# The second group of a pointwise convolution: two of its eight pairs by seven products

## The chip, the cores and the metric

The kernel runs on one core of one Trainium2 chip. The metric is the device time of one execution in microseconds; the median of several is taken. Beside it stands one execution recorded by the hardware profiler, whose span goes from the first instruction to the last.

## What is computed

One layer of a hybrid encoder block in float32, for 256 tokens and a model width of 4096. Cut to what matters here:

```python
proj = rms_norm(x) @ w_in                       # 4096 -> 14336: q k v z_a a_c g_c z_c
y_a  = rms_norm(chunked_attention(q, k, v)) * silu(z_a)
u    = silu(layer_norm(depthwise_conv(a_c * sigmoid(g_c))))
y_c  = rms_norm(u @ w_pw + b_pw) * silu(z_c)    # w_pw: 2048 x 2048, the pointwise convolution
h    = x + concat(y_a, y_c) @ w_out
h    = h + sigmoid(rms_norm(h) @ w_ple_gate + b) * (p @ w_ple)
out  = rms_norm(h)
```

The change lies in `u @ w_pw + b_pw`.

## The kernel before

**Products.** Every float32 operand is split into a high part (a cast, on ScalarE, L204) and a low part (a subtraction on VectorE, L205). A product of a block of 128 activations by 128 x 512 weights is three matmuls on TensorE: high by high, low by high, high by low.

**Groups and pairs.** `mixed_product` (L340 on) computes a group: two halves of tokens (h = 0, 1) by two stretches of 512 columns (j = 0, 1), in four accumulator banks. It goes over the contraction in pairs of 128-row blocks, in the order that `order` gives. For a *plain* pair, both blocks are multiplied into all four banks: 2 x 4 x 3 = 24 matmuls. For a pair marked `*`, the 2 x 2 x 2 block product is done with seven products instead of eight (L452 to L488): 7 x 3 = 21 matmuls. It needs sums of the weights (ua at L465 and L466, ub at L472 and L473, on VectorE), the parts of these sums (uh on ScalarE, ul on VectorE), and sums of the activations that are made beforehand, here called combinations (`combine_again`, L287; its last steps are L276 on ScalarE and L277 on VectorE). P1 and three helper products, P5, P6 and P7, go into four helper banks, and when the last such pair of a group is through, `on_helpers` adds them up (L509 to L513, and lines of the caller).

**Buffers.** Weights arrive by SyncE's queue in five buffers `w`; wh and wl have three each, ua/ub, uh and ul two each. The queue issues a load when VectorE has read the tile that held the buffer before.

**The pointwise convolution.** L996 to L1032: two groups (columns 0 to 1023 and 1024 to 2047), eight pairs each. The activations are uS[0] to uS[3], two pairs in each. uC holds the combinations of pairs 0 and 2, made ahead of the first group. The first group takes pairs 0 and 2 by seven products; the second takes all pairs plain and has no helper sums, so it adds the bias with the last sums (L1030).

**What follows.** `xS` (L1037 on) are six more combinations, of the normalised input, for the gate groups that come next (order `dense`: 1 0\* 3 2\* 5 4\* 6\* 7 8\* ...). Their tiles xS[1] to xS[3] come from the pool `more`, whose four tiles are uS[0] to uS[3], so each waits until the second pointwise group is done with one of these.

**Order of the work.** The order of instructions on each engine is made at compile time: an instruction goes when its operands and its buffers are free in the compiler's model of the time, and among those that can go, the earlier line of the program goes first. Each engine then works through its list in that order. Only the instructions under `pin` keep the order of the program, and there are none of these around the change.

Of the kernel before, what the change touches and what calls it, by code (L numbers as in the profile page):

```python
# [25 lines left out]
def hybrid_block(  # L26
# [297 lines left out]
    def units(text):  # L324

        return [(int(u.rstrip("*+")), u[-1] if u[-1] in "*+" else "") for u in text.split()]
# [666 lines left out]

    fill(len(later))

    point = units("1 3 4 5 0* 6 2* 7"), units("0 1 2 3 4 5 6 7")  # L996
    uC = {}
    for c in range(2):
        uC[2 * c] = act.tile([P, 2, 2, T], F32R, tag="act", name="comb_u"), 0
# [339 lines left out]
```

## Time and profile before

| | |
|---|---|
| median of 3 runs | 2033.08 us (2032.29 to 2034.44) |
| profiled execution | 2032.83 us, span 2031.1 us |
| granted TensorE clock | 0.998 of full |
| first pointwise group | about 900 to 947 us |
| second pointwise group | about 947 to 990.5 us |
| first gate group | from 991.0 us |

Times in the views are microseconds from the start of the span. PE is TensorE, PEld its weight loads, DVE VectorE, ACT ScalarE, SP SyncE. A line of the timeline has start, duration, engine, line of the kernel, operation, output and inputs, and in brackets how long the engine sat idle before it and what ended that. L204 and L205 are helpers that every weight tile goes through; the names tell which tile it is: wh and wl of the weights, uh and ul of their sums.

### The profile page before, as it was taken

Reading aid. Unit: us, or ns where it says so; the run is one execution under the profiler, and the core shown is the slowest. Engines: PE = TensorE matmul, PEld = TensorE weight load, DVE = VectorE, ACT = ScalarE, POOL = GpSimd, SP = SyncE. Lnnn points to the kernel's source line nnn. Section 1 sums busy time; section 2 is a strip of 40 time slices with the busy share of each in tenths; the row PEclk is TensorE's granted clock in tenths of the full one; section 3 lists DMA queues with packets and bytes.
Section 4 is the critical chain, followed back from the end, with each engine's and each line's share of the span. In section 5 each row is a group of like instructions: output and inputs, shape, how many; then the busy total and the mean of one; then the engine's idle time right before and its main releaser. Section 6 shows DMA issues by size and latency. Waiting matters only on the chain.

```text
span 2031.1 us, 26144 instructions
## 1 busy us (share of the span) xinstructions
PE 2015.5 (99%) x9094; PEld 1658.7 (82%) x9094; DVE 1871.1 (92%) x2658; ACT 1203.3 (59%) x1568; POOL 46.0 (2%) x50
## 2 busy tenths in 40 slices
PE   9999999999999999999999999999999999999997
PEld 7888888888888888888888888888888888888876
DVE  7999999679999986868899999999999999999998
ACT  7655555655655445676556566675665666665555
POOL 0000000000000000000000000000000000000000
PEclk9999999999999999999999999999999999999999
DMA  8787878688678867556666666676666656666765
GB/s 294 223 237 233 257 214 251 191 245 239 188 217 250 254 187 207 171 185 205 194 214 198 202 205 214 217 229 209 206 213 201 208 187 207 204 220 205 234 208 179
DMA packets 171167, 436.69 MB, mean 215 GB/s; under 512 B 13966, under 2 KB 17182, under 8 KB 171034
## 3 DMA queue, kind: packets, MB, share of 16 engines
q1 hardware_dynamic: 161952, 417.93, 64.0%
q0 software_dynamic: 8432, 16.25, 4.9%
q8 instruction: 71, 1.16, 0.2%
q10 hardware_dynamic: 650, 0.84, 0.1%
q14 instruction: 62, 0.51, 0.1%
HBM read 430.77 MB, written 4.19 MB: 214 GB/s over the span
## 4 chain that ended last, share of the span: by engine, by line
PE 92%; DVE 5%; issue 2%; ACT 1%; DMA 1%; POOLq 0%; POOL 0%; ACTq 0%; DVEq 0%
PE acc L383 67%; PE acc_P L383 16%; PE acc L229 5%; DVE wl L205 2%; PE tmp_ps L170 1%; DVE cv L721 1%; DMA wt<-in_w_out_dram 0%; PE tmp_ps L890 0%; DVE ul L205 0%; PE tmp_ps L874 0%; PE tmp_ps L908 0%; PE tmp_ps L913 0%; ACT wh L204 0%; PE acc L371 0%; DVE cv L799 0%
## 5 line engine op out<-in xcount | busy, mean ns | idle before, releaser
L383 PE MATMUL acc<-wh,big_t 128*128 128x512 f32 x3992 | 1234.7, 391 | 0.7 <-DVE y_c L1030 0.3
L204 ACT CAST wh<-wt 128x1024 fp32r<-128x1024 f32 (+1 forms) x737 | 713.4, 978 | 550.5 <-PE acc L383 365.0
L205 DVE TENSOR_TENSOR wl<-wt,wh 128x1024 fp32r<-128x1024 f32 (+1 forms) x737 | 821.8, 1127 | 82.0 <-ACT wh L204 78.6
L383 PEld LDWEIGHTS acc<-wh,big_t 128*128 128x128 f32 x3992 | 746.8, 188 | 155.1 <-issue 0.9
L383 PE MATMUL acc<-wl,big_t 128*128 128x512 f32 x1996 | 770.7, 391 | 0.6 <-DVE wl L205 0.5
L383 PEld LDWEIGHTS acc<-wl,big_t 128*128 128x128 f32 x1996 | 374.3, 188 | 79.5 <-DVE wl L205 2.3
L204 ACT CAST uh<-ua 128x1024 fp32r<-128x1024 f32 x160 | 168.3, 1052 | 80.9 <-DVE ua L466 46.1
L721 DVE SCALAR_TENSOR_TENSOR cv<-uT,dw,cv 128x250 f32<-128x250 f32 (+19 forms) x480 | 202.3, 463 | 1.1
L205 DVE TENSOR_TENSOR ul<-ua,uh 128x1024 fp32r<-128x1024 f32 x160 | 194.9, 1218 | 8.4 <-ACT uh L204 8.0
L383 PE MATMUL acc_P<-uh,big_t 128*128 128x512 f32 x516 | 157.9, 391 | 0.0
L204 ACT CAST uh<-ub 128x1024 fp32r<-128x1024 f32 x92 | 96.8, 1053 | 95.8 <-DVE ub L473 86.5
L205 DVE TENSOR_TENSOR ul<-ub,uh 128x1024 fp32r<-128x1024 f32 x92 | 112.2, 1220 | 6.1 <-ACT uh L204 5.2
L383 PEld LDWEIGHTS acc_P<-uh,big_t 128*128 128x128 f32 x516 | 95.8, 188 | 22.3 <-ACT uh L204 3.1
L383 PE MATMUL acc_P<-ul,big_t 128*128 128x512 f32 x258 | 98.8, 391 | 0.1
L229 PE MATMUL acc<-wh,big_t 128*128 128x512 f32 x304 | 93.9, 390 | 0.0
L465 DVE TENSOR_TENSOR ua<-wt 128x512 f32<-128x512 f32 x95 | 65.1, 685 | 18.3 <-DMA wt<-in_w_in_dram 12.4
L383 PE MATMUL acc<-uh,big_t 128*128 128x512 f32 x252 | 78.1, 390 | 0.0
L383 PE MATMUL acc_P<-wh,big_t 128*128 128x512 f32 x252 | 77.8, 389 | 0.0
L229 PEld LDWEIGHTS acc<-wh,big_t 128*128 128x128 f32 x304 | 56.9, 188 | 11.9 <-issue 0.2
L383 PE MATMUL acc_P<-uh,comb_t 128*128 128x512 f32 x216 | 66.4, 390 | 0.1
L466 DVE TENSOR_TENSOR ua<-wt 128x512 f32<-128x512 f32 x95 | 64.9, 683 | 1.1 <-DMA wt<-in_w_in_dram 1.1
L473 DVE TENSOR_TENSOR ub<-ub,wt 128x512 f32<-128x512 f32 x92 | 63.0, 685 | 0.8
(250 smaller groups left out, 1589.3 us busy)
## 6 DMA issues: line engine op xcount, KB each, us to landing
wt<-in_w_in_dram SPq DMA_DIRECT2D x416, 512.0 KB, 4.5
wt<-in_w_out_dram SPq DMA_DIRECT2D x128, 512.0 KB, 4.3
wt<-in_w_ple_gate_dram SPq DMA_DIRECT2D x128, 512.0 KB, 4.2
wt<-in_w_pw_dram SPq DMA_DIRECT2D x32, 512.0 KB, 4.7
ua<-in_w_in_dram SPq DMA_DIRECT2D x31, 512.0 KB, 4.2
ua<-in_w_in_dram POOLq DMA_DIRECT2D x31, 512.0 KB, 8.3
wt<-in_w_in_dram SPq DMA_DIRECT2D x31, 256.0 KB, 2.7
hc<-in_x_dram SPq DMA_DIRECT2D x8, 512.0 KB, 4.8
```

Source lines behind the costliest of these rows:

```text
L170: nc.tensor.transpose(pt[:, i * T + h * P : i * T + (h + 1) * P], src[:, h, b] if len(src.shape) == 4 else src[:, h, b * P : (b + 1) * P], ...
L204: nc.scalar.copy(wh[:, :kc, :], wt[:, :kc, :]),
L205: nc.vector.tensor_tensor(wl[:, :kc, :], wt[:, :kc, :], wh[:, :kc, :].bitcast(F32), ALU.subtract),
L229: nc.tensor.matmul(acc, a, b[:, k, :], start=kb == 0 and kind == 0, stop=kb == kblocks - 1 and kind == 2,)
L383: nc.tensor.matmul(banks[name], a, b, start=name not in begun, stop=final and ends[name] == n and kind == 2 and not (left and name in "P2 ...
L465: plus(ua[:, 0], w0[:, 0], w0[:, 1])
L466: plus(ua[:, 1], w0[:, 1], w1[:, 1])
L473: plus(ub[:, 1], ub[:, 0], w1[:, 0])
L721: nc.vector.scalar_tensor_tensor(cv[:, i, PAD - k :], uT[:, i, : T + k - PAD], dw[:, b, k : k + 1], cv[:, i, PAD - k :], ALU.mult, ALU.add,)
```

## The change

The second group is given the same order as the first. It takes pairs 0 and 2 by seven products and the other six plain, in the order 1 3 4 5 0\* 6 2\* 7, on the combinations that are in uC for the first group already. With that the group has helper banks and helper sums, so it takes the branch of L1028 in place of L1030.

```diff
-    point = units("1 3 4 5 0* 6 2* 7"), units("0 1 2 3 4 5 6 7")
+    point = (units("1 3 4 5 0* 6 2* 7"),) * 2
```

## The prediction

> **What bounds the kernel now.** I read the page's busy times first, then a table by stretches around the changed stage, the waits of TensorE there, and the chain.
>
> ```profile
> PE 2015.5 (99%) x9094; PEld 1658.7 (82%) x9094; DVE 1871.1 (92%) x2658; ACT 1203.3 (59%) x1568; POOL 46.0 (2%) x50
> 945.00:991.00 46.00, 45.71 (x202) 37.37 (x200) 37.91 (x58) 26.43 (x36) 0.00 (x0) 1.00 0.62 193
> 991.00:1073.00 82.00, 81.72 (x358) 67.06 (x359) 75.11 (x90) 49.15 (x57) 0.69 (x1) 1.00 0.63 201
> 1073.00:1155.00 82.00, 82.00 (x362) 67.73 (x362) 78.33 (x94) 49.38 (x55) 0.00 (x0) 1.00 0.64 206
> ```
>
> The rows of the table give length, then busy time and count of PE, PEld, DVE, ACT and POOL, the granted clock, and the DMA. The first is about the second pointwise group, the second the first gate group, the third the next one. TensorE is occupied throughout at full clock, so a matmul less is a gain and a wait of TensorE is a loss. VectorE is the runner-up: 37.9 of 46 us in the changed stage, 75.1 and 78.3 of 82 behind it. ScalarE, with 26.4 of 46, has room.
>
> ```profile
> PE acc L383 <- DVE y_c L1030: 0.3, 1, 0.3
> PE acc L383 <- DVE z L1054: 0.2, 1, 0.2
> 940.30 38.63 PE acc L383 x170
> 990.32 0.39 PE L383 MATMUL acc<-wl,big_t 128*128 128x512 f32 x1
> 991.04 0.73 PE L383 MATMUL acc<-wh,big_t 128*128 128x512 f32 x2 [0.33 <-DVE y_c L1030]
> 999.37 0.62 PE L383 MATMUL acc_P<-uh,comb_t 128*128 128x512 f32 x2
> ```
>
> The two waits are all that TensorE waited for between 945 and 1075. The chain's row gives the price of a matmul: 38.63 / 170 = 0.227 us from start to start (the 0.39 us of a row is a pipelined latency). The last matmul of the second group starts at 990.32 and the gate group at 991.04, 0.49 us later than the cadence. The last row is product P6 of gate pair 0\*, the first seven-product pair behind the group; I measure the lag there. Its third matmul, at 999.37 + 0.45 = 999.82, is the first that reads ul of ub.
>
> **TensorE's part.** A plain pair has 2 blocks x 4 banks x 3 = 24 matmuls, 5.45 us; by seven products 7 x 3 = 21, 4.77 us. Two pairs save 6 x 0.227 = 1.36 us, all on the bound engine. The gap of 0.49 us may go too, so no more than 1.85 us can be gained here.
>
> **VectorE's part.** Prices are from start to start in its gapless stretches:
>
> ```profile
> 1009.29 2.35 DVE L205 TENSOR_TENSOR wl<-wt,wh 128x1024 fp32r<-128x1024 f32 x2
> 1011.57 1.22 DVE L205 TENSOR_TENSOR ul<-ua,uh 128x1024 fp32r<-128x1024 f32 x1
> 1012.70 0.68 DVE L205 TENSOR_TENSOR wl<-wt,wh 128x512 fp32r<-128x512 f32 x1
> 1013.30 0.68 DVE L473 TENSOR_TENSOR ub<-ub,wt 128x512 f32<-128x512 f32 x1
> 1013.90 0.68 DVE L465 TENSOR_TENSOR ua<-wt 128x512 f32<-128x512 f32 x1
> 940.48 0.68 DVE L510 TENSOR_TENSOR y_c<-acc_P,y_c 128x512 f32<-128x512 f32 x1
> 943.01 0.68 DVE L512 TENSOR_TENSOR y_c<-acc_P,y_c 128x512 f32<-128x512 f32 x1
> 943.62 0.68 DVE L1020 TENSOR_TENSOR y_c<-y_c,row 128x512 f32<-128x512 f32 x1
> 944.22 0.68 DVE L513 TENSOR_TENSOR y_c<-acc_P,y_c 128x512 f32<-128x512 f32 x1
> 945.41 1.28 DVE L1020 TENSOR_TENSOR y_c<-y_c,row 128x512 f32<-128x512 f32 x2
> ```
>
> A 1024-wide subtraction takes 1.14 us (two in 2.28), a 512-wide one or an addition 0.60. Per seven-product pair the four additions (L465, L466, L472, L473) come in, 2.40, and two ul, 2.28; one wl shrinks from 1024 to 512 columns, -0.54: 4.14 us, and 8.28 for two pairs. The helper sums come in once: L1017, L510 to L513 and three of L1020, 8 x 0.60 = 4.80, as the first group's rows show. The four last sums stay (L1028 for L1030). Together 13.1 us more on VectorE.
>
> [...]
>
> How much of 13.1 us finds idle time? From 948 until ul of ub of gate 0\* is written, these are all the idle times of VectorE that the timeline lists, and the row that ends the stretch (1.22 from 995.61, so 996.83):
>
> ```profile
> 955.57 1.23 DVE L205 TENSOR_TENSOR wl<-wt,wh 128x1024 fp32r<-128x1024 f32 x1 [1.28 <-ACT wh L204]
> 958.29 1.23 DVE L205 TENSOR_TENSOR wl<-wt,wh 128x1024 fp32r<-128x1024 f32 x1 [1.50 <-ACT wh L204]
> 959.43 1.28 DVE L277 TENSOR_TENSOR big_t<-comb,big_t 128x512 fp32r<-128x512 f32 x2
> 966.45 1.22 DVE L205 TENSOR_TENSOR wl<-wt,wh 128x1024 fp32r<-128x1024 f32 x1 [0.24 <-ACT wh L204]
> 969.17 1.23 DVE L205 TENSOR_TENSOR wl<-wt,wh 128x1024 fp32r<-128x1024 f32 x1 [1.50 <-ACT wh L204]
> 970.31 1.29 DVE L277 TENSOR_TENSOR big_t<-comb,big_t 128x512 fp32r<-128x512 f32 x2
> 973.27 0.69 DVE L291 TENSOR_TENSOR comb<-big_t 128x512 f32<-128x512 f32 x1
> 977.33 1.22 DVE L205 TENSOR_TENSOR wl<-wt,wh 128x1024 fp32r<-128x1024 f32 x1 [0.97 <-ACT wh L204]
> 980.04 1.23 DVE L205 TENSOR_TENSOR wl<-wt,wh 128x1024 fp32r<-128x1024 f32 x1 [1.50 <-ACT wh L204]
> 981.19 1.29 DVE L277 TENSOR_TENSOR big_t<-comb,big_t 128x512 fp32r<-128x512 f32 x2
> 985.09 0.69 DVE L466 TENSOR_TENSOR ua<-wt 128x512 f32<-128x512 f32 x1 [0.88 <-DMA wt<-in_w_in_dram]
> 993.86 0.69 DVE L465 TENSOR_TENSOR ua<-wt 128x512 f32<-128x512 f32 x1 [0.15 <-DMA wt<-in_w_in_dram]
> 995.61 1.22 DVE L205 TENSOR_TENSOR ul<-ub,uh 128x1024 fp32r<-128x1024 f32 x1
> ```
>
> They come to 8.02 us. Not all can be had, because of the order of the pairs. Between its waits VectorE also makes the six combinations of x for the gate groups, and the three rows of L277 are their last steps. Each pair of them needs a tile that uS gives back. With 8 x 5.45 = 43.6 us ending at 990.55 the group starts at 946.9; pairs 0 and 1 are done at 957.8, 2 and 3 at 968.7, 4 and 5 at 979.6, and L277 follows each by 1.6 us. In the new order the first tile to come free is uS[2], when 1, 3, 4 and 5 are done (968.7); then uS[0] after 0\* (973.5) and uS[1] after 2\* (983.7). So what VectorE did of combinations ahead of 968.7 (959.43 to 966.21 less two wl of 1.14: 4.5 us) moves behind that time, while the new 4.14 us for 0\* come in ahead of it. These nearly cancel, and the first three idle times (1.28 + 1.50 + 0.24 = 3.02) stay. The other five, 5.0 us, are used up, since from 968.7 on there is always something ready: the preparation of 2\*, the last four combinations and all six last steps, the helper sums.
>
> I take the full 13.1 - 5.0 = 8.1 us of delay for ul of ub: 996.83 + 8.1 = 1004.9 against the 999.82 at which TensorE wanted it, 5.1 us late. It includes the 1.36 us, because TensorE now waits for VectorE and its own path is no longer the one that counts. The bounds, with the lead of 3.0 us that ul has now (999.82 - 996.83): with all 8.02 us used, 13.1 - 8.0 - 3.0 = +2.1 us; with none, 13.1 - 3.0 = +10.1. I choose the middle, since the weights of 0\* can be there early while the combinations cannot.
>
> Does TensorE win it back? No: its busy time is 81.72 of 82 and then 82.00 of 82, so it has nothing to give. Nor does it lose more: from 0\* to 6\* VectorE needs two plain and three seven-product pairs, 2 x 2.28 + 3 x 6.42 = 23.8 us, TensorE 25.2.
>
> The remaining edits cost nothing on the path. ScalarE gets two casts uh for half a wh per pair and one copy:
>
> ```profile
> 989.92 0.60 ACT L204 CAST wh<-wt 128x512 fp32r<-128x512 f32 x1
> 994.16 1.04 ACT L204 CAST uh<-ub 128x1024 fp32r<-128x1024 f32 x1
> SPq L438 <- DVE wl L205: 38.9, 16, 6.9
> ```
>
> That is about 2 x (2 x 1.04 - 0.44) + 0.6 = 3.9 us against 19.6 idle; without that room they would delay each ul behind them. Transfers are as many and as large as before, issued in the new order of pairs. Their queue waits for VectorE to free weight buffers (the last row, 945 to 1000), so a late VectorE delays the loads too, but five buffers hold two and a half pairs. Combinations for pairs 0 and 2 exist already. The new y tiles need slots that uC holds until 2\* is done, which is when their sums can start anyway.
>
> **The rivals.**
> (A) The forecast, +5.1 us; its own range is +2.1 to +7.1, from 8.0 down to 3.0 us of idle time found.
> (B) The backlog is absorbed. The combinations of pairs 12 and 14 are wanted only late in the gate group, and one costs 0.60 + about 1.0 + 0.60 = 2.2 us (973.27 to the next step is 0.60, two of L277 take 1.20; the small steps are an estimate). If the compile-time order puts all of the last four behind gate 0\*, 8.8 us leave the path and 5.1 turns to the gain of TensorE alone, -1.36 to -1.85; with two of them, +0.7. For: 6.9 us of VectorE are unused between 991 and 1073. Against: the rows show L277 running as soon as its tile is free, ahead of gate work, so the earlier line of the program goes first.
> (C) VectorE does not close its gaps: each of its steps waits for a cast behind other casts, or for weights that left the queue late. At most 3 of the 8.0 us are found and the delay is +7.1 to +10.1, 2040.2 to 2043.2. The gate 0\* has a wait for weights already (0.88). Against: 940 to 949, in the first group, has no such gap.
> (D) The wait falls in one piece and the clock drops:
>
> ```profile
> 2020.00:2022.00 2.00, 0.00 (x0) 0.00 (x0) 1.79 (x5) 0.51 (x2) 0.73 (x1) 1.00 0.54 204
> 2022.00:2024.00 2.00, 0.00 (x0) 0.00 (x0) 1.68 (x4) 1.76 (x3) 0.20 (x1) 0.69 0.09 34
> ```
>
> At the end, where TensorE has stopped, the clock is still 1.00 up to 2022 and falls to 0.69 in the next 2 us, so a pause of some 4 us is needed. If half clock then lasted 4.3 us (an estimate, as long as it took to come), 2.1 us are added: 2040.3. [...] Against (D): the lag comes in steps of single tiles of 1.1 us, between which TensorE works.
> That the change does nothing can't be: the order string alone decides which pairs go by seven products.
>
> **How the numbers follow.** The profiled execution took 2032.83 us (span 2031.1), the median is 2033.08. With +5.1 they become 2037.9 and 2038.2; I forecast 2038.2. 0.2% is 4.07 us, about what a measurement can tell. Chances: A 0.57, of which 0.39 above 4.07; B 0.27, all within; C 0.12 and D 0.04, both above. Slower 0.55, within 0.44, faster 0.01, as the gain ends at 1.85 us. B must lie in the range, so it starts at -1.85 (2031.2); the upper end cuts C at +8.9 (2042.0), leaving out some 0.05.
>
> **What would show it.** Right: 6 matmuls and the 1.36 us fewer; VectorE without gaps from about 969 to 1005; L277 at about 970, 975 and 985; P6 of gate 0\* near 1004.5, then no further lag, and waits of TensorE for wl or ul of about 6 us between 984 and 1005. Wrong: L277 of the last two combinations behind 1000 and no such waits (B), VectorE idle behind 969 (C), a granted clock under 1 (D), or a lag that shrinks later.

## The result, and the profile after

The changed kernel takes 2037.81 us (median of 12 runs, 2036.63 to 2039.90) against 2033.40 (12 runs): 1.0022 times as long, 95% interval 1.0014 to 1.0030, that is 4.4 us more. The forecast was 5.1 us more. The profiled execution took 2036.92 us (span 2035.1).

First the page's line of busy times:

```profile
PE 2017.0 (99%) x9088; PEld 1657.9 (81%) x9088; DVE 1883.9 (93%) x2678; ACT 1206.8 (59%) x1573; POOL 49.0 (2%) x50
```

Three rows of the table by stretches, in the columns explained before:

```profile
945.00:991.00 46.00, 43.93 (x194) 35.90 (x193) 41.11 (x60) 27.24 (x37) 0.00 (x0) 1.00 0.55 181
991.00:1073.00 82.00, 80.91 (x343) 64.87 (x344) 80.01 (x104) 48.34 (x59) 3.61 (x1) 0.98 0.65 200
1073.00:1155.00 82.00, 82.00 (x363) 67.56 (x362) 78.85 (x94) 49.64 (x55) 0.00 (x0) 1.00 0.65 205
```

The 6 matmuls are gone (9088 for 9094), and VectorE is busy 12.8 us longer (1883.9 for 1871.1; 13.1 was forecast). TensorE has more idle time than before in the first two rows (2.07 of 46 us and 1.09 of 82, where 0.29 and 0.28 were), and the clock is below 1 in the second. From 1073 on TensorE is busy throughout, as before. The waits of TensorE between 945 and 1075 (total, count, longest, in us):

```profile
PE acc L383 <- DVE y_c L1028: 2.1, 1, 2.1
PE acc_P L383 <- ACT uh L204: 0.9, 1, 0.9
PE acc L383 <- DVE wl L205: 0.2, 1, 0.2
```

TensorE's timeline where they fall (start, duration, idle time ahead and what ended it in brackets):

```profile
988.46 0.39 PE L383 MATMUL acc<-wl,big_t 128*128 128x512 f32 x1
990.92 0.95 PE L383 MATMUL acc<-wh,big_t 128*128 128x512 f32 x2 [2.07 <-DVE y_c L1028]
999.66 0.61 PE L383 MATMUL acc<-wh,big_t 128*128 128x512 f32 x2
1001.13 1.21 PE L383 MATMUL acc_P<-uh,comb_t 128*128 128x512 f32 x4 [0.86 <-ACT uh L204]
1004.87 0.96 PE L383 MATMUL acc<-wl,big_t 128*128 128x512 f32 x3 [0.23 <-DVE wl L205]
1006.82 0.62 PE L383 MATMUL acc_P<-uh,comb_t 128*128 128x512 f32 x2
```

And the table by stretches around the first of them, the clock third from the end:

```profile
990.00:991.00 1.00, 0.07 (x1) 0.10 (x1) 1.00 (x3) 0.19 (x1) 0.00 (x0) 1.00 0.00 0
991.00:992.00 1.00, 1.00 (x3) 0.84 (x4) 1.00 (x3) 0.97 (x3) 0.00 (x0) 0.60 0.00 0
992.00:994.00 2.00, 2.00 (x6) 1.52 (x6) 2.00 (x3) 1.74 (x6) 0.00 (x0) 0.50 0.00 0
994.00:995.00 1.00, 1.00 (x5) 0.78 (x4) 1.00 (x6) 0.00 (x0) 0.27 (x1) 0.69 0.00 0
```

The largest wait is at the change of banks: the gate group starts 990.92 - 988.46 - 0.23 = 2.23 us late (0.49 before), because the last sums (L1028) that empty the accumulators come late. Then the clock runs at half speed (the 0.50 of the third row) for 3.4 us: 0.8 of the second row, all 2.0 of the third, 0.6 of the last, worth 1.7 us of matmuls. Then TensorE waits 1001.13 - 999.66 - 0.45 = 1.02 us for uh of gate 0\*, and 0.4 us for a wl. With the gain: -1.36 + (2.23 - 0.49) + 1.7 + 1.0 + 0.4 = +3.5 us. That is where the time went, not yet why. ScalarE, which casts uh, had itself waited for VectorE's sum ua, as its timeline shows:

```profile
1000.04 1.04 ACT L204 CAST uh<-ua 128x1024 fp32r<-128x1024 f32 x1 [0.41 <-DVE ua L466]
```

The four last sums of the first gate group (start and duration first, last number the count) show the same lag. VectorE's timeline of the kernel before:

```profile
1071.99 2.47 DVE L1054 TENSOR_TENSOR z<-acc,z 128x512 f32<-128x512 f32 x4
```

And of the changed kernel:

```profile
1075.69 2.48 DVE L1054 TENSOR_TENSOR z<-acc,z 128x512 f32<-128x512 f32 x4
```

They lag by 3.7 us, of which 0.15 is there ahead of the change already; at the last matmuls of the kernel it is 4.1. VectorE's timeline, cut to the idle times that end behind 955, four of the six last steps of the combinations (L277; the other two start at 977.63 and 997.71), the last sums and ul of ub of gate 0\* (1007.08):

```profile
955.75 1.23 DVE L205 TENSOR_TENSOR wl<-wt,wh 128x1024 fp32r<-128x1024 f32 x1 [1.31 <-ACT wh L204]
957.26 0.69 DVE L465 TENSOR_TENSOR ua<-wt 128x512 f32<-128x512 f32 x1 [0.29 <-DMA wt<-in_w_pw_dram]
959.33 0.69 DVE L466 TENSOR_TENSOR ua<-wt 128x512 f32<-128x512 f32 x1 [1.37 <-DMA wt<-in_w_pw_dram]
965.75 1.23 DVE L205 TENSOR_TENSOR ul<-ub,uh 128x1024 fp32r<-128x1024 f32 x1 [0.52 <-ACT uh L204]
967.83 0.69 DVE L465 TENSOR_TENSOR ua<-wt 128x512 f32<-128x512 f32 x1 [0.86 <-DMA wt<-in_w_pw_dram]
970.07 0.69 DVE L466 TENSOR_TENSOR ua<-wt 128x512 f32<-128x512 f32 x1 [0.41 <-DMA wt<-in_w_pw_dram]
975.89 0.68 DVE L277 TENSOR_TENSOR big_t<-comb,big_t 128x512 fp32r<-128x512 f32 x1
...
984.29 0.68 DVE L277 TENSOR_TENSOR big_t<-comb,big_t 128x512 fp32r<-128x512 f32 x1
...
987.69 0.68 DVE L513 TENSOR_TENSOR y_c<-acc_P,y_c 128x512 f32<-128x512 f32 x1
988.29 0.68 DVE L277 TENSOR_TENSOR big_t<-comb,big_t 128x512 fp32r<-128x512 f32 x1
988.89 1.28 DVE L1020 TENSOR_TENSOR y_c<-y_c,row 128x512 f32<-128x512 f32 x2
990.10 2.47 DVE L1028 TENSOR_TENSOR y_c<-acc,y_c 128x512 f32<-128x512 f32 x4
...
1002.40 0.68 DVE L277 TENSOR_TENSOR big_t<-comb,big_t 128x512 fp32r<-128x512 f32 x1
...
1007.08 1.21 DVE L205 TENSOR_TENSOR ul<-ub,uh 128x1024 fp32r<-128x1024 f32 x1
...
1023.16 1.23 DVE L205 TENSOR_TENSOR ul<-ub,uh 128x1024 fp32r<-128x1024 f32 x1 [0.19 <-ACT uh L204]
```

Behind 970.1 the view lists no idle time of VectorE for 53 us; up to 1005, where TensorE's last wait ends, it is the engine that sets the pace.

### The profile page after: what moved, and what is told of

Read it like the earlier page. It is cut to its first block, busy times and chain, and to the rows that moved or that the text cites. A ratio compares the mean times of both kernels' runs of the same rounds, so it can differ in the third digit from the quotient of the medians.

```text
span 2035.1 us, 26149 instructions
## 1 busy us (share of the span) xinstructions
PE 2017.0 (99%) x9088; PEld 1657.9 (81%) x9088; DVE 1883.9 (93%) x2678; ACT 1206.8 (59%) x1573; POOL 49.0 (2%) x50
## 4 chain that ended last, share of the span: by engine, by line
PE 94%; DVE 4%; issue 1%; ACT 0%; POOLq 0%; POOL 0%; ACTq 0%; DVEq 0%
PE acc L383 69%; PE acc_P L383 17%; PE acc L229 5%; DVE wl L205 1%; PE tmp_ps L170 1%; DVE cv L721 1%; PE tmp_ps L890 0%; PE tmp_ps L874 0%; PE tmp_ps L908 0%; PE tmp_ps L913 0%; PE acc L371 0%; DVE cv L799 0%; PE tmp_ps L889 0%; PE tmp_ps L125 0%; PE tmp_ps L915 0%
```

## The experiments

Three readings stood against each other. *Backlog*: 13.1 us of added VectorE work do not fit into its idle time, and TensorE pays the rest. *Late tiles*: the new order of pairs returns the uS tiles later. *Banks*: only the wait of 2.2 us and the low clock behind it cost, and both hang on where the helper sums stand. Differences are to the kernel before on the same chip (median 2033.25 to 2033.35); intervals are 95%.

**The new order alone.** Edit to the changed kernel:

```diff
-    point = (units("1 3 4 5 0* 6 2* 7"),) * 2
+    point = units("1 3 4 5 0* 6 2* 7"), units("1 3 4 5 0 6 2 7")
```

> The second group in the new order of pairs (1 3 4 5 0 6 2 7), but all eight pairs plain: the late return of the uS tiles without any added VectorE work. Backlog theory (the 13.1 us of added VectorE work do not fit): no lag, within 0.5 us of 2033.4. Rival, late tiles (the combinations of x that are held up by uS come too late, the added work itself would fit): most of the loss stays, 2036 or more.

2033.20 us, 0.9999 [0.9990, 1.0008]. The late return costs nothing by itself; late tiles is out as the only cause.

**The seven-product pairs early.** `units("1 0* 3 2* 4 5 6 7")` for the second group.

> The second group in the order 1 0* 3 2* 4 5 6 7: the same added VectorE work and the same 6 matmuls fewer, but the uS tiles come back as before the change and the helper sums lie four plain pairs ahead of the change of banks. Backlog theory in its strict form (only the amount counts, 13.1 against at most 8.0 us idle and 3.0 us of lead): +2.1 us, 2035.5. Bank theory (the loss is the wait of 2.2 us for the last sums behind the helper sums, with the clock that falls after it): no wait, the gain of 1.4 us, 2032.0. Late tiles: 2032.0 too.

2034.55 us, 1.0007 [0.9998, 1.0016]: +1.2 us, between the two times, and not clear of noise. The wait at the second change of banks is gone, as banks says, but one row of TensorE shows that the last sums are late at the first change instead, where VectorE has the first group's own helper sums (the last of them at 946.67) and now the preparation of 0\* too:

```profile
948.10 0.70 PE L383 MATMUL acc<-wh,big_t 128*128 128x512 f32 x2 [1.03 <-DVE y_c L1028]
```

**The combinations later.** The combinations for pairs 8, 10, 12 and 14 go into the work that `fill` hands out between the gate pairs:

```diff
     for c in range(2, D // NB):
         if c % 2 == 0:
             comb_tile(xS, 1)
-        combine_again(xS[c // 2], 2 * (c % 2), xT[c], 0, sum_rows())()
+        if c < 4:
+            combine_again(xS[c // 2], 2 * (c % 2), xT[c], 0, sum_rows())()
+        else:
+            later.extend(combination_later(c))   # its two steps, as two callables
```

> The changed kernel, but the combinations of x for pairs 8, 10, 12 and 14 are made between the pairs of the first gate group instead of ahead of it (8.8 us of VectorE by the forecast's estimate). Backlog theory: the lag of 4.4 us goes to the gain, 2032 to 2033. Bank theory: only the two last steps (1.2 us) and small ones leave the helper sums' stretch; the wait falls from 2.2 to about 1 us and the clock stays up, 2034.5.

2037.12 us, 1.0018 [1.0009, 1.0027]: +3.8 us. A miss for both. The edit did less than was meant: in the compile-time order one of the four combinations stayed ahead of the gate group, with its last step at 983.95 (984.29 in the changed kernel); the last steps of the other three went from 988.29, 997.71 and 1002.40 to 1002.87, 1007.83 and 1017.49. TensorE's timeline in this run, its first matmul of the gate group:

```profile
990.11 0.70 PE L383 MATMUL acc<-wh,big_t 128*128 128x512 f32 x2 [1.22 <-DVE y_c L1028]
```

The table by stretches, around that matmul and further on:

```profile
990.00:996.00 6.00, 5.89 (x25) 4.62 (x26) 5.96 (x11) 5.31 (x12) 0.95 (x1) 1.00 0.14 22
1020.00:1030.00 10.00, 8.96 (x37) 6.43 (x36) 10.00 (x12) 5.64 (x6) 0.00 (x0) 1.00 0.50 148
```

VectorE's last sums of the first gate group (L1065 here):

```profile
1074.51 2.48 DVE L1065 TENSOR_TENSOR z<-acc,z 128x512 f32<-128x512 f32 x4
```

The pause is shorter and the clock stays at 1.00. But preparation for gate pairs has taken the place of the combinations in VectorE's order, and the postponed work comes up to 1018, ahead of the preparation that TensorE wants next: it idles 1.0 us of 10 behind 1020, with VectorE busy in all 10. The lag at the gate group's last sums is 2.5 us. That it is 3.9 us at the last matmuls of this profile was not traced further.

**The same move in the kernel before.**

> The kernel before the change, with only the move of the run before: the combinations of x for pairs 8, 10, 12 and 14 are made between the pairs of the first gate group. No seven-product pair is added. Backlog theory: VectorE loses 8.8 us of work in a stretch where it then idles, and gets it where it had 2.6 us idle and 3.0 of lead, so 2 to 3 us are lost, 2035.5 to 2036.5. Rival (room in the gate group, as the 6.9 us unused between 991 and 1073 suggest): 2033.4.

2033.84 us, 1.0001 [0.9992, 1.0011]. This run tests nothing. The program makes the four combinations later, but the compile-time order left them where they were. VectorE's timeline has all six last steps ahead of the gate group, each 0.7 us later than before, like the first addition of a combination ahead of them (L291, 953.18 for 952.45), and its order from 950 to 1010 is that of the kernel before:

```profile
960.14 1.29 DVE L277 TENSOR_TENSOR big_t<-comb,big_t 128x512 fp32r<-128x512 f32 x2
971.02 1.28 DVE L277 TENSOR_TENSOR big_t<-comb,big_t 128x512 fp32r<-128x512 f32 x2
981.90 1.28 DVE L277 TENSOR_TENSOR big_t<-comb,big_t 128x512 fp32r<-128x512 f32 x2
```

Whether the gate group has room for 8.8 us more stays open.

**No helper sums.** In the second group `on_helpers` returns at once, so the output lacks these products.

> The changed kernel, but the second group leaves out the helper sums: its four helper products are computed and not added, the bias goes in with the last sums as before the change. VectorE has 4.8 us less to do, all of it just ahead of the change of banks. Bank theory: the wait of 2.2 us and the low clock go, 4.4 - 1.7 - 1.7 = +1.0, 2034.4. Backlog theory: 13.1 - 4.8 = 8.3 us against 5.0 us idle and 3.0 of lead, 2033.5 to 2034. Late tiles: 2036 or more. All in one: if it stays above 2036, both of the first two are wrong.

2032.97 us, 0.9999 [0.9990, 1.0008], below the times of all three readings: 4.8 us of VectorE work taken away bring 4.8 us back against the changed kernel. The run takes away the work and its place at once, so it does not tell amount from place.

**Fewer combinations.** The four combinations of the earlier run are left out, and the gate groups read others in their place, so the output is another one.

> The changed kernel without the combinations of x for pairs 8, 10, 12 and 14 (the gate groups read those of 4 and 6 in their place): 8.8 us less on VectorE, not moved but gone. Backlog theory: the lag goes and the gain of the 6 matmuls shows, about 2032.0 to 2032.5. If the lag were a matter of the last sums' place in the order alone, the wait at the change of banks would stay as it was with the combinations moved (1.2 us), and the time at 2035 to 2037.

2031.57 us, 0.9991 [0.9982, 0.9999]: 1.7 us faster than before, within its interval the gain of the 6 matmuls (1.36) and the pause that TensorE no longer makes. Here the helper sums stand where they stand in the changed kernel, and the same row shows what is left of the wait:

```profile
989.93 0.70 PE L383 MATMUL acc<-wh,big_t 128*128 128x512 f32 x2 [0.42 <-DVE y_c L1028]
```

So the place of the sums alone does not make the wait; it takes the amount of work on VectorE around them. (ScalarE loses four casts here too, but where TensorE waited for uh, ScalarE was itself waiting for VectorE.)

**One seven-product pair.** `units("1 3 4 5 0* 6 2 7")`.

> The second group with one seven-product pair in place of two (1 3 4 5 0* 6 2 7): three matmuls fewer (0.7 us), and 4.1 + 4.8 = 8.9 us more on VectorE. Backlog theory: 8.9 against 5.0 idle and 3.0 of lead, +0.9, less the 0.7 us by which it was too high before: 2033.3 to 2034.3. If the loss came with the seven-product pairs one by one (2.2 us each), 2035.5.

2032.54 us, 0.9997 [0.9988, 1.0006], a little below the range of the backlog theory. The added 8.9 us of VectorE work fit; the loss does not come pair by pair. But the helper sums start at 969.16 here, as soon as 0\* is through, and at 981.42 in the changed kernel, so this run moves their place too and does not tell amount from place.

**TensorE kept busy.** 14 matmuls of 128 x 128 with no use, between the two groups:

```diff
         y_c.extend(ys)
+    hot = tmp_psum()
+    for _ in range(14):
+        nc.tensor.matmul(hot[:, :P], ident, ident, start=True, stop=True)
```

> The changed kernel with 14 small matmuls of no use between the last matmul of the second pointwise group and the first of the gate group, so that TensorE is not idle at the change of banks and its clock has no reason to fall. If the clock costs what its records show (1.7 us), 2036.1. Backlog theory: TensorE only waits that much longer for uh of gate 0*, whose time VectorE sets; no change, 2037.5 to 2038.

2038.19 us, 1.0026 [1.0017, 1.0034]. They took 3.3 us, longer than the pause, so a second run has 9:

> The changed kernel with 9 small matmuls of no use at the change of banks instead of the 14 of an earlier run, which took 3.3 us, 0.8 more than the pause they were to fill. 9 of them take about 2.1 us and fit into the pause of 2.2 us. Backlog theory: the clock stays up and the time with it, 2037.5 to 2038: TensorE waits that much longer for VectorE. If the clock costs what its records show (1.7 us): 2036.1.

2037.93 us, 1.0023 [1.0014, 1.0032], as the changed kernel. The rows of this run: the 9 (18 in the profile's count) fit the pause, the clock stays at 1.00, and TensorE waits 0.76 and 1.03 us a little later. The table by stretches:

```profile
986.00:992.00 6.00, 6.00 (x36) 5.10 (x35) 6.00 (x12) 3.02 (x6) 0.00 (x0) 1.00 0.33 129
992.00:996.00 4.00, 3.24 (x13) 1.93 (x13) 4.00 (x11) 3.12 (x7) 0.94 (x1) 1.00 0.16 16
```

TensorE's timeline:

```profile
989.13 2.17 PE L1035 MATMUL tmp_ps<-ident 128*128 128x128 f32 x18
994.69 1.20 PE L383 MATMUL acc<-wl,big_t 128*128 128x512 f32 x4 [0.76 <-DVE wl L205]
1001.46 1.19 PE L383 MATMUL acc_P<-uh,comb_t 128*128 128x512 f32 x4 [1.03 <-ACT uh L204]
```

So the low clock costs nothing on the path: without it TensorE waits for VectorE instead.

**The seven-product pairs in the middle.** `units("1 3 0* 4 2* 5 6 7")`.

> The second group in the order 1 3 0* 4 2* 5 6 7: the same work as in the changed kernel, the seven-product pairs away from both changes of banks, the uS tiles back after the third, fifth and sixth pair. Backlog theory: the idle time ahead of 969 can be used, so 13.1 against 8.0 and 3.0, less the 0.7 us by which the theory was too high so far: +1.4, 2034.8. Bank theory: no wait at either change, the gain of 1.4 us, 2032.0.

2032.91 us, 0.9998 [0.9989, 1.0007]. All the 13.1 us are there, and the lag of 4.4 us is not. The time is nearer to the one of banks (2032.0) than to the one of backlog (2034.8). The table by stretches of the changed kernel:

```profile
945.00:969.00 24.00, 24.00 (x107) 19.68 (x107) 19.59 (x26) 14.76 (x21) 0.00 (x0) 1.00 0.57 192
969.00:991.00 22.00, 19.93 (x89) 16.22 (x87) 21.53 (x35) 12.48 (x17) 0.00 (x0) 1.00 0.53 169
```

And of this one:

```profile
945.00:969.00 24.00, 24.00 (x107) 19.74 (x106) 23.81 (x32) 17.74 (x25) 0.00 (x0) 1.00 0.60 200
969.00:991.00 22.00, 22.00 (x98) 18.21 (x98) 21.88 (x38) 12.23 (x19) 0.00 (x0) 1.00 0.60 185
```

VectorE, the third busy time, works 23.8 of 24 us ahead of 969 instead of 19.6: 4.2 us that are idle there in the changed kernel are used, about as much as the lag. The helper sums also stand earlier (L1017 to L513 start at 969.15 to 976.17, in the changed kernel at 981.42 to 987.69), so the run shows that the same work costs nothing when it is done earlier; whether the idle time used or the place of the sums does it, it does not tell. This is the version to prefer over the change. Its profile shows no wait of TensorE between 930 and 1100, yet the runs do not separate it from the kernel before.

**Combinations on GpSimd.** The sums for the four combinations go to GpSimd, as plain additions and subtractions; their last steps stay.

> The changed kernel with the sums for the combinations of x of pairs 8, 10, 12 and 14 on GpSimd, which is idle there; only their last step (L277) stays on VectorE. About 4 x 1.6 = 6.4 us less for VectorE, the output as before. Backlog theory: 13.1 - 6.4 = 6.7 us fit, the lag goes and the gain shows, 2032.0 to 2032.5, unless GpSimd makes a combination so slowly that the last step is late. If GpSimd's work slows VectorE, 2034 to 2036.

2043.53 us, 1.0052 [1.0039, 1.0064]: a miss, 10.3 us slower than before and 5.7 slower than the changed kernel. The waits between 969 and 1005:

```profile
ACT big_t L283 <- POOL comb L272: 15.5, 3, 5.6
DVE big_t L284 <- ACT big_t L283: 6.5, 2, 3.6
PE acc L390 <- DVE y_c L1035: 3.6, 1, 3.6
```

ScalarE's cast of the combination (L283 here) waits for GpSimd, and the casts wh and uh queue behind it; VectorE, relieved of work, then waits for ScalarE. This run says nothing against the backlog theory, and nothing for it.

**What decides.** Two runs separate the readings: with fewer combinations the helper sums keep their place and the loss goes, and with TensorE kept busy the clock keeps its speed (1.00) and the loss stays. So VectorE's load between 970 and 1005 makes the loss, and the low clock does not. As a sum, added work against idle time and lead, the backlog theory was poor: 0.4 to 1.9 us too high in five runs and 4.1 too low with the combinations later. How many us fit, and how much of that hangs on where the sums stand, is not settled.

## Why the prediction was right, point by point

**TensorE's part** held: 6 matmuls, and 1.4 us that show once VectorE is relieved (1.7 us with fewer combinations).

**VectorE's part** held: 13.1 us forecast, 12.8 measured. Its start-to-start prices (0.60 and 1.14 us) were the better ones: by the durations of the rows (0.68 and 1.22) the same sum is 2 x (4 x 0.68 + 2 x 1.22 - 0.54) + 8 x 0.68 = 14.7 us, 1.9 too much.

**The idle time** held in kind. That the idle times ahead of 969 cannot be used, since uS comes back late, was the step on which the size hung: 3.0 us forecast, 4.4 measured (1.31 + 0.29 + 1.37 + 0.52 + 0.86), and behind 970.1 no more idle time, as forecast. Up to ul of ub 4.8 us stay idle, with the 0.41 at 970.07, where 8.0 were before: 3.3 us were used, not 5.0. The run with the pairs in the middle uses the idle times, and the lag goes. The new order alone costs nothing; only with the added work does it bind. That it is uS which keeps these times empty is argued, since no run changes its return alone with the added work in place.

**Where TensorE pays** was wrong. I measured the lag at P6 of gate 0\* and let ul of ub set it. ul was written at 1008.3, not 1004.9: of the 3.4 us, 1.7 are the idle time that was not found, and the rest should be other work that the compile-time order put ahead of it (worked out, not traced). Yet TensorE never waited for ul: that order put matmuls of gate pair 3 ahead of P6, so TensorE worked meanwhile, and P6 at 1006.82 is 7.4 us later than before while the lag is 3.7. Of the forecast 6 us of waits for wl or ul, 0.2 came; 2.1 were for y_c and 0.9 for uh. The step that failed is the one that kept the order of products fixed. By the forecast's own rule ul at 1008.3 would have cost 1008.3 - 999.8 = 8.5 us; that 5.1 came so near to 4.4 is in part luck, two errors against each other.

**The change of banks** I priced at nothing (the 0.49 us "may go"); it became 2.23 us. L1028 reads what the helper sums leave, so these 4.8 us lie ahead of the four last sums, and steps of combinations lie between them (988.29). What I called unchanged had gained a wait in front.

**(B)** fell: L277 does run later than forecast (975.9 to 1002.4 for 970 to 985), and two of the last four combinations end behind the change of banks, but the lag stayed, and postponing three of them on purpose moved it instead of removing it. **(C)** fell by its sign, as VectorE closed its gaps behind 970.1. By its amount it was nearer than (A): the 3.3 us used are close to its "at most 3", and 2.9 of the 4.8 us left end with a weight load (0.29 + 1.37 + 0.86 + 0.41). **(D)** came to pass in a way not foreseen: I wanted a pause of some 4 us (at the end of the kernel before, TensorE stopped at 2018.5 and the clock fell between 2022 and 2024), and here 2.23 us was enough. The half clock lasted 3.4 us, 4.3 by my estimate. My price of about 2 us was right for TensorE's own time (1.7 us) and wrong for the path (nothing, as the runs that kept TensorE busy show). Whether the length of a pause alone decides, no run here tests.

**Recovery.** As forecast, nothing is won back later: 3.7 us at the first gate group's end, 4.1 at the last matmuls.

## What to carry to other kernels

When a trade takes work from the bound engine and gives more to the runner-up, add up the runner-up's idle time only over the stretch where the new work can be done and its results are wanted: here 8.9 us fitted, 13.1 us did not, and the same 13.1 us fitted when placed two pairs earlier (in both runs that fitted, the helper sums came earlier as well). The wait that the profile shows (banks, casts, a low clock) is then only the place where a backlog surfaces: filling the pause moved it, and taking work away or placing it earlier removed it. And look in the trace whether a moved line has moved the work: with an order made at compile time, one such edit here left VectorE's order as it was.

## What the runs showed of the hardware

A pause of TensorE of 2.23 us was followed by 3.4 us at half clock (0.50), and filled with matmuls it was not (1.00 in both runs that filled it); pauses of 1.38 us (combinations later, 990.11 - 988.50 - 0.23) and 1.0 us (changed kernel, 1001.13) left the clock at 1.00. In the GpSimd run some steps of VectorE and GpSimd took longer where they ran side by side: a 512-wide addition on VectorE, 0.69 us elsewhere, took 1.78, and GpSimd's own took 2.15 where it took 1.27 with VectorE idle (VectorE's gap of 3.60 us ends at 988.14). The timelines of the two:

```profile
985.77 1.27 POOL L298 TENSOR_TENSOR comb<-big_t 128x512 f32<-128x512 f32 x1
991.29 2.15 POOL L298 TENSOR_TENSOR comb<-big_t 128x512 f32<-128x512 f32 x1
992.21 1.78 DVE L472 TENSOR_TENSOR ua<-wt 128x512 f32<-128x512 f32 x1
```

How much of the 5.7 us that this run is slower than the changed kernel comes from this, how much from ScalarE's queue and how much from the clock, which was low as well (0.89 in the mean of 969 to 988, 0.50 from 988 to 990), was not separated.
